# Two more modulation blocks as dot products, head norms and softmax rows scaled by ScalarE, and a new placing of side work

## The chip, the cores and the metric

The kernel runs on one core of one Trainium2 chip. The time is device microseconds of one execution. Three timed executions of the kernel before took 1323.88, 1324.15 and 1324.64 us, so the median is 1324.15 us. The profile comes from a fourth execution of its own.

The core has TensorE (PE for matmuls, PEld for their weight loads), VectorE (DVE), ScalarE (ACT), GpSimd (POOL) and SyncE (SP), which issues most of the loads. Each engine works through its own instructions in the order in which they stand and stops at the first one whose inputs or buffers are not there.

## What is computed

One layer of a diffusion backbone, for two groups of 128 tokens ("prompt" and "sample"), model width 2048. A conditioning vector per group gives six modulation vectors. The core of the reference:

```python
sh1, sc1, g1, sh2, sc2, g2 = ada_mod(c[:, None, :], w_ada[l], b_ada[l])   # split(silu(c) @ w_ada + b_ada, 6)
h = rms_norm(xs, norm1_w[l]) * (1 + sc1) + sh1
qa, ka, va, qb, kb, vb, ga, gb = project_heads(h, ...)    # h @ w_in, then rms_norm of every q and k head
qa, ka = axial_rope(qa, T), axial_rope(ka, T)             # sample group only
oa = latent_window_attention(qa, ka, va, cache_a_k, cache_a_v, sink)
ob = latent_neighbourhood_attention(qb, kb, vb, cache_b_k, cache_b_v, rpb_b)
xs = xs + g1 * merge_branches(oa, ob, ga, gb, w_br_a, w_br_b, w_out)
h2 = rms_norm(xs, norm2_w[l]) * (1 + sc2) + sh2
xs = xs + g2 * sq_relu_mlp(h2, w_up[l], w_down[l])
```

The prompt group runs through the same steps with plain attention over its own 128 tokens. Everything is 32-bit floating point.

## The kernel before

**Steps.** The large products (w_in, w_br_a, w_br_b, w_out, w_up, w_down) run as 456 steps in one list, `wsteps`. A step loads one 512 KB piece of a weight (`raw`, 128x1024). To keep the precision, the piece is split into a high part and a rest: ScalarE copies `raw` into `wH` (line 101), VectorE subtracts `wH` from `raw` into `wL` (line 260). TensorE then multiplies in threes, high by high, low by high and high by low. Outside the fast form of w_up a step has 12 matmuls of 512 columns. Steps 0 to 71 make q, k and v, 72 to 135 the gates, 136 to 167 the two branch products, 168 to 199 w_out, and the rest w_up and w_down.

**What sets the order.** Nothing is scheduled by itself. `run()` writes the instructions out step by step. The strings `RUN` and `LOOK` have one digit per step: how many steps ahead of the matmuls the load is issued, and how many ahead the split is written. All other work has step numbers in tables at the head of the file (`POST`, `JOBS`, `DOTS`, `DOTS2`, `DOTS1`, `SS_AT`, `T_PAIR`, `P_PAIR`), and is written behind the matmuls of that step. So a table entry decides where a piece of side work stands among the splits on ScalarE and VectorE. Tiles of 128x1024 come from one pool of 50 buffers.

**Splits with a DMA.** For the steps listed in `LO_DMA` VectorE does not make the rest. ScalarE writes minus `wH` into `wL` (line 266) and GpSimd issues a DMA that adds the weight from memory once more (line 267).

**Modulation.** The shift and scale of a norm are needed as columns. Each vector is 16 blocks of 128 columns, and a block can be made in two ways.
- As matmuls, in pairs of blocks: `pair_load` fetches 2 MB per block, `pair_mm` (line 330) issues 16 small matmuls per block, `ada_evac` copies the result out with ScalarE, `ada_cols` turns it with four PE transposes (line 348) and finishes with small VectorE operations (lines 351 to 358). For the second norm the blocks 0 to `FB_DVE`-1 go this way, at the steps in `SS_AT`.
- As dot products on VectorE: `dot` (line 1411) multiplies a transposed weight tile (`aT`, 512 KB) by the conditioning row spread over the partitions (`cB`), and sums. A block of shift and scale is 2 vectors x 2 halves x 2 groups, so 8 such operations and four loads. `DOTS` places these for gate 1 and for the second norm's blocks from `FB_DVE` on, `DOTS1` those of the first norm's last two blocks, `DOTS2` those of gate 2.

**Head norms.** `qk_stat` squares a unit of q or k heads on ScalarE, one instruction per group, and VectorE sums per head (line 673). GpSimd makes the inverse roots. `qk_apply` scales the prompt group's heads one by one on ScalarE (line 683) and the sample group's with one VectorE multiply (line 684). VectorE then applies the norm weight (686) and the rotary (693 to 696), and `qk_T` turns the result for the scores. There are six units of 4 heads per group and one (`kvA`) of 2. `POST` has the three steps of each.

**Softmax.** There are eight attention jobs, each of four heads and one group, with 128 keys per row for the prompt and 256 for the sample. `normalise` (line 795) divides the four heads' rows by their sums with one VectorE multiply. `JOBS` has the five steps of each job: scores, softmax, normalise, turning, values.

**The last steps.** `up_act`, `up_planes`, `up_flip` and `up_T` square the result of w_up, cut it into 16-bit planes, turn it with a transposing DMA and join it (`fTa`, then `a14H`, `a14L` for the last unit but one). `P_PAIR` and `T_PAIR` place them.

Of the kernel before, what the change touches and what calls it, by code (L numbers as in the profile page):

```python
# [14 lines left out]
AF = mybir.ActivationFunctionType  # L15
OP = mybir.AluOpType
AX = mybir.AxisListType

P = 128
D = 2048  # L20
KC = D // P
HD = 128
# [7 lines left out]
PIECES = [[2 * i, 2 * i + 1] for i in range(8)]  # L30
GEN = 50
LOAD = 4
FB_DVE = 6
FB1 = 14
H_AT = 41
DOTS1 = [26, 26, 29, 36, 39, 40, 41, 42]
CHUNKS = [2, 2, 2, 4, 6]
NFAST = 8
FAST = {1: (0, 2, 3, 5, 6, 7), 2: (0, 2, 3, 5, 6, 7), 3: (0, 2, 3, 5, 6, 7), 4: (0, 2, 3, 5, 6, 7), 5: (0, 2, 3, 5, 6, 7), 6: (0, 2, 3, 5, 6, 7), 7: (0, 2, 3, 5, 6, 7)}
# [8 lines left out]
GATE2_USE = 3  # L48
ROW_AT = [5, 5, 9, 5]
DIRECT = (3,)  # L50
LO_DMA = [88, 106, 116, 131, 165, 180, 184, 196, 218, 224, 230, 232, 250, 251, 256, 282, 283, 288, 314, 315, 320, 329, 346, 347, 352, 378, 379, 384, 392, 410, 416, 442, 443, 449, 450]
LO_AHEAD = 2

LOOK = "652322414122454322223333333122333442223323122555465644344534355765215632223444456685566655544323333333321122122312343545666445443333342344444444444434556566643344457766322234414766567565566546555331235663226676666666656665554444444444444444555555555555555544433333333344445555555555555555444444444444444455555555555555554444433244444444555555555555555546444444444444445555555555555555444444444445555555666465555555554444446656654585434443744464222433444444"
RUN = "411111111111121323334444433333333312222233465566655466545667777556664445555776765655445445555656776654432333333312444444555566553333333343334455555566655655555655666575565577788866677666665653476544343366555566666666666666665555555555554444566666666666666655555555555555556666666666666666555555555555555566666666555666665555577555555555666666666666666655555555555555556666666666666666555577755555575454566666676555566666666665555555776766555535444666666666"
CONST_AT = [65, 69]
ADA_AT = [None, 5, 13, 16, 21, 37, 32]
XS_AT = {1: 13, 2: 19, 3: 31}
POST = {('kvA', 0): [67, 71, 76], ('qA', 0): [70, 73, 78], ('qA', 1): [72, 74, 83], ('kB', 0): [76, 86, 90], ('qB', 0): [82, 84, 93], ('kB', 1): [87, 90, 98], ('qB', 1): [90, 93, 96]}
JOBS = [[80, 81, 81, 88, 94], [79, 83, 88, 90, 92], [87, 87, 89, 95, 100], [93, 93, 96, 102, 105], [96, 97, 100, 105, 112], [102, 103, 107, 112, 123], [105, 107, 111, 118, 123], [112, 115, 118, 121, 123]]  # L60
SS_AT = [44, 57, 75, 75, 139, 139]
T_AT = [3, 4]
PREP_IN = [5, 7]
DOTS = [32, 44, 47, 47, 49, 50, 51, 52, 53, 56, 58, 60, 67, 67, 68, 69, 77, 78, 84, 85, 92, 93, 93, 94, 95, 99, 100, 103, 103, 104, 108, 110, 111, 111, 116, 118, 120, 120, 121, 122, 126, 126, 128, 129, 130, 132, 134, 137, 137, 138, 138, 143, 144, 145, 151, 155, 155, 158, 160, 160, 166, 167, 173, 173, 174, 175, 176, 178, 179, 180, 183, 190]
DOTS2 = [234, 237, 240, 266, 269, 272, 298, 301, 329, 330, 332, 363, 364, 367, 397, 398, 424, 426, 426, 428, 429, 431, 431, 432, 432, 436, 439, 439, 440, 441, 444, 444]
STAT_AT = [-1, 0, 8, 11]
T_PAIR = [[6, 8], [6, 8], [8, 10], [5, 7], [10, 13], [8, 14], [12, 9]]
P_PAIR = [[1, 3], [2, 4], [3, 4], [-1, 3], [3, 4], [3, 6], [6, 4]]
M_TE = (3,)
M_AT = [1, 3, 8]  # L70
FLIP = 2
P_UP = [2, 3]
T_UP = [6, 11]
COL = {"qA": 0, "kvA": 1024, "qB": 1536, "kB": 2560, "vB": 3584, "gA": 4608, "gB": 6656}


# [1 line left out]
def tile_hybrid_step(ctx: ExitStack, tc: tile.TileContext, a):  # L78
# [98 lines left out]
    r = SM(2, "r")  # L177
# [489 lines left out]
    def qk_stat(u, nh):  # L667
        raw = units[u]
        sq = G("sq").rearrange("p (s h d) -> p s h d", s=2, d=HD)[:, :, 0:nh, :]
        for s in range(2):  # L670
            act.activation(sq[:, s].rearrange("p h d -> p (h d)"), raw[:, s, 0:nh * HD], AF.Square)
        ssq, r = SM(2 * nh, "ssq"), SM(2 * nh, "rq")
        dve.tensor_reduce(ssq.rearrange("p (s h) -> p s h", s=2), sq, axis=AX.X, op=OP.add)
        rsqrt(r, ssq, HD * EPS)
        qk[u] = sq, r

    def qk_apply(u, nh):

        name, raw = u[0], units[u]
        x4 = raw.rearrange("p s (h d) -> p s h d", d=HD)[:, :, 0:nh, :]  # L680
        sq, r = qk.pop(u)
        for h in range(nh):
            act.activation(x4[:, 0, h, :], x4[:, 0, h, :], AF.Copy, scale=r[:, h:h + 1])
        dve.tensor_tensor(x4[:, 1], x4[:, 1], r[:, nh:2 * nh].unsqueeze(2).to_broadcast([P, nh, HD]), op=OP.mult)
        if name in ("kvA", "kB"):
            dve.tensor_tensor(x4[:, 0], x4[:, 0], K2["wb"][name].unsqueeze(1).to_broadcast([P, nh, HD]), op=OP.mult)
        if name in ("qA", "kvA"):
# [44 lines left out]
    def att_job(mix, s, g):  # L732
        st = {}
        nb = 1 + s
        nk = P * nb
# [53 lines left out]
        def normalise():  # L789
            den, prob = st["den"], st["P"]  # L790
            if mix == "A":
                dve.tensor_tensor(den, den, st["es"], op=OP.add)
            rd = SM(4, "rd")
            dve.reciprocal(rd, den)
            dve.tensor_tensor(prob[:, :, 0:nk], prob[:, :, 0:nk], rd.unsqueeze(2).to_broadcast([P, 4, nk]), op=OP.mult)

        def probs_T():
            st["PT"] = G("probT").rearrange("p (b h q) -> p b h q", b=2, h=4)
# [808 lines left out]
```

## Time and profile before

| | us |
|---|---|
| median of three timed executions | 1324.15 |
| the profiled execution, its own time | 1324.28 |
| its span in the trace | 1322.5 |
| TensorE matmul busy | 1309.0 |
| VectorE busy | 1151.4 |
| ScalarE busy | 890.8 |
| GpSimd busy | 87.1 |

The span is 1.8 us shorter than the execution's own time. Busy times are sums over the span and say nothing about who waits for whom, since the stages differ: loads take the DMA engines' whole time for the first 200 us, VectorE is fullest between 160 and 260 us and between 1220 and 1300 us, and ScalarE between 920 and 1010 us and in the w_up stages. Matmul records overlap: one is shown for 390 ns, while the next begins after about 227 ns.

### The profile page before, as it was taken

What the parts mean: (1) busy time and instruction counts of PE and PEld (TensorE: products, weight loads), DVE (VectorE), ACT (ScalarE), POOL (GpSimd) and SP (SyncE); (2) the same over time, 40 slices, a digit from 0 to 9 for tenths busy, and PEclk for the clock granted to TensorE, in tenths of its full rate; (3) what the DMA queues carried; (4) which work ended last, traced back from release to release, by engine and by line L of the source; (5) the groups of instructions that cost most, each with busy time, mean ns of one, the idle gap of its engine ahead of it and who ended that gap; (6) DMA issues with size and microseconds to landing.
All of it is one profiled execution on the core that took longest, in us unless ns stands there. A gap on an engine that the chain in (4) does not pass through costs nothing.

```text
span 1322.5 us, 18220 instructions
## 1 busy us (share of the span) xinstructions
PE 1309.0 (99%) x6388; PEld 1061.3 (80%) x6388; DVE 1151.4 (87%) x1487; ACT 890.8 (67%) x1129; POOL 87.1 (7%) x109
## 2 busy tenths in 40 slices
PE   8999999999999999999999999999999999999998
PEld 4777788788888878888888888888888888888876
DVE  4578699988898999999789889898898998979996
ACT  5634656576565545755788877968879688796772
POOL 0000000512000000000100010100101001010011
PEclk9999999999999999999999999999999999999999
DMA  9999998887689999998489998888998799899996
GB/s 375 408 408 409 406 398 344 326 286 281 200 296 343 373 377 349 323 374 306 137 289 291 290 312 273 283 300 289 292 321 281 282 341 288 295 269 366 375 334 185
DMA packets 155260, 419.03 MB, mean 317 GB/s; under 512 B 52720, under 2 KB 53984, under 8 KB 155168
## 3 DMA queue, kind: packets, MB, share of 16 engines
q1 hardware_dynamic: 146128, 386.54, 80.1%
q0 software_dynamic: 8848, 31.23, 10.3%
q8 instruction: 50, 0.82, 0.2%
q14 instruction: 42, 0.34, 0.1%
q10 hardware_dynamic: 192, 0.10, 0.0%
HBM read 390.24 MB, written 17.61 MB: 308 GB/s over the span
## 4 chain that ended last, share of the span: by engine, by line
PE 93%; DMA 3%; DVE 2%; issue 1%; POOL 0%; ACT 0%; POOLq 0%; DVEq 0%; ACTq 0%
PE acc L313 16%; PE acc L314 16%; PE acc L315 16%; PE Q L1191 6%; PE Q L1192 6%; PE Q L1193 6%; PE acc L424 5%; PE acc L425 5%; PE acc L426 5%; PE ps_ada L330 2%; DMA araw<-in_w_pair 2%; PE ps_S L756 1%; DMA wL<-in_w_down 1%; DVE aT L1411 1%; PE acc L1026 1%
## 5 line engine op out<-in xcount | busy, mean ns | idle before, releaser
L101 ACT ACTIVATE wH<-raw 128x1024 fp32r<-128x1024 f32 (+1 forms) x376 | 381.0, 1045 | 126.4 <-DMA raw<-in_w_in 17.0
L260 DVE TENSOR_TENSOR wL<-raw,wH 128x1024 fp32r<-128x1024 f32 x335 | 399.1, 1223 | 47.8 <-ACT wH L101 32.7
L424 PE MATMUL acc<-wH,hH 128*128 128x512 f32 x276 | 109.1, 395 | 0.0
L426 PE MATMUL acc<-wH,hL 128*128 128x512 f32 x276 | 107.6, 390 | 0.0
L425 PE MATMUL acc<-wL,hH 128*128 128x512 f32 x276 | 107.5, 390 | 0.0
L313 PE MATMUL acc<-wH,hH 128*128 128x512 f32 x256 | 102.6, 401 | 0.0
L315 PE MATMUL acc<-wH,hL 128*128 128x512 f32 x256 | 99.8, 390 | 0.0
L314 PE MATMUL acc<-wL,hH 128*128 128x512 f32 x256 | 99.7, 390 | 0.0
L1411 DVE CUSTOM_DVE_ANT_0 junk<-aT,cB,cols 128x1024 bf16<-128x1024 f32 x56 | 71.3, 1283 | 1.4 <-DMA cB<-silu 1.4
L1411 DVE CUSTOM_DVE_ANT_0 aT<-aT,cB,cols 128x1024 f32<-128x1024 f32 x56 | 71.6, 1288 | 0.2
L424 PEld LDWEIGHTS acc<-wH,hH 128*128 128x128 f32 x276 | 51.8, 188 | 13.6 <-issue 3.3
L1256 DVE TENSOR_TENSOR tL<-t,tH 128x1024 fp32r<-128x1024 f32 x42 | 51.2, 1220 | 11.2 <-ACT tH L101 11.2
L426 PEld LDWEIGHTS acc<-wH,hL 128*128 128x128 f32 x276 | 51.8, 188 | 11.2 <-DVE hL L105 0.2
L101 ACT ACTIVATE uH<-raw 128x1024 fp32r<-128x1024 f32 x42 | 44.4, 1058 | 23.6 <-DVE raw L1250 21.5
L425 PEld LDWEIGHTS acc<-wL,hH 128*128 128x128 f32 x276 | 51.9, 188 | 10.3
L101 ACT ACTIVATE tH<-t 128x1024 fp32r<-128x1024 f32 x42 | 44.3, 1054 | 23.5 <-DVE t L1246 18.5
L313 PEld LDWEIGHTS acc<-wH,hH 128*128 128x128 f32 x256 | 48.1, 188 | 10.5 <-issue 1.1
L314 PEld LDWEIGHTS acc<-wL,hH 128*128 128x128 f32 x256 | 48.1, 188 | 10.0 <-issue 0.7
L315 PEld LDWEIGHTS acc<-wH,hL 128*128 128x128 f32 x256 | 48.1, 188 | 10.1
L1246 DVE TENSOR_TENSOR t<-raw 128x1024 f32<-128x1024 f32 x42 | 51.2, 1218 | 1.0 <-PE acc L314 1.0
L1238 DVE TENSOR_TENSOR XL<-raw,XH 128x1024 fp32r<-128x1024 f32 x42 | 51.2, 1218 | 0.6 <-DMA sm<-dsum 0.5
L1256 DVE TENSOR_TENSOR uL<-raw,uH 128x1024 fp32r<-128x1024 f32 x42 | 51.1, 1218 | 0.0
(630 smaller groups left out, 3374.4 us busy)
## 6 DMA issues: line engine op xcount, KB each, us to landing
raw<-in_w_in SPq DMA_DIRECT2D x133, 512.0 KB, 9.0
raw<-in_w_down SPq DMA_DIRECT2D x128, 512.0 KB, 6.6
raw<-in_w_upF SPq DMA_DIRECT2D x84, 512.0 KB, 6.3
araw<-in_w_pair SPq DMA_DIRECT2D x80, 512.0 KB, 10.1
aT<-in_w_gT SPq DMA_DIRECT2D x64, 512.0 KB, 8.9
aT<-in_w_adaT SPq DMA_DIRECT2D x48, 512.0 KB, 9.9
raw<-in_w_up SPq DMA_DIRECT2D x44, 512.0 KB, 6.2
raw<-in_w_out SPq DMA_DIRECT2D x32, 512.0 KB, 10.2
```

Source lines behind the costliest of these rows:

```text
L101: act.activation(out, in_, AF.Copy)
L260: dve.tensor_tensor(st["lo"], st["raw"], st["hi"].bitcast(F32), op=OP.subtract)
L313: pe.matmul(acc[tb], sh, wh[:, k, :], start=f, stop=False, **kw)
L314: pe.matmul(acc[tb], sh, wl[:, k, :], start=False, stop=False, **kw)
L315: pe.matmul(acc[tb], sl, wh[:, k, :], start=False, stop=l, **kw)
L424: pe.matmul(acc[tb], sh, wh[:, k, :], start=kt == 0 and k == 0 and not held and not seeded, stop=False, **kw)
L425: pe.matmul(acc[tb], sh, wl[:, k, :], start=False, stop=False, **kw)
L426: pe.matmul(acc[tb], sl, wh[:, k, :], start=False, stop=last and k == 1 and not hold, **kw)
L1191: pe.matmul(acc, stat[0], hi, start=f, stop=False)
L1192: pe.matmul(acc, stat[0], lo, start=False, stop=False)
L1256: dve.tensor_tensor(b[n + "L"], v, b[n + "H"].bitcast(F32), op=OP.subtract)
L1411: dve.tensor_tensor_reduce(out, box["raw"], cB[s, tag], 1.0, dst if second else baT[:, part, fb:fb + 1], OP.mult, OP.add, dst)
```

## The change

The second norm's blocks made by matmuls go from 6 to 4, so blocks 4 and 5 become dot products: 32 small matmuls, 4 transposes, one ScalarE copy, four small VectorE operations and 4 MB of loads go, and 16 dot products with 8 loads of 512 KB come. The squares of the head norms are taken head by head on ScalarE with the sum as a second output, and the VectorE sums go. The sample group's heads and the softmax rows are scaled by ScalarE, head by head. `LO_DMA` has 33 entries in place of 35. The strings `LOOK` and `RUN` differ in some places (the first of them is shown, cut), and most tables by a few entries.

```diff
-FB_DVE = 6
+FB_DVE = 4
-DOTS1 = [26, 26, 29, 36, 39, 40, 41, 42]
+DOTS1 = [26, 29, 34, 35, 35, 36, 39, 42]
-LO_DMA = [88, 106, 116, 131, 165, 180, 184, 196, 218, 224, 230, 232, 250, 251, 256, 282, 283, 288, 314, 315, 320, 329, 346, 347, 352, 378, 379, 384, 392, 410, 416, 442, 443, 449, 450]
+LO_DMA = [57, 92, 106, 114, 116, 127, 165, 172, 184, 196, 224, 232, 237, 256, 282, 283, 288, 314, 315, 320, 329, 346, 347, 352, 378, 379, 384, 385, 410, 416, 440, 442, 449]
-POST = {('kvA', 0): [67, 71, 76], ('qA', 0): [70, 73, 78], ('qA', 1): [72, 74, 83], ('kB', 0): [76, 86, 90], ('qB', 0): [82, 84, 93], ('kB', 1): [87, 90, 98], ('qB', 1): [90, 93, 96]}
+POST = {('kvA', 0): [67, 71, 76], ('qA', 0): [70, 73, 78], ('qA', 1): [72, 74, 83], ('kB', 0): [76, 86, 90], ('qB', 0): [80, 84, 93], ('kB', 1): [87, 91, 99], ('qB', 1): [90, 93, 96]}
-SS_AT = [44, 57, 75, 75, 139, 139]
+SS_AT = [75, 75, 139, 139]
-DOTS = [32, 44, 47, 47, 49, 50, 51, 52, 53, 56, 58, 60, 67, 67, 68, 69, 77, 78, 84, ...]
+DOTS = [43, 44, 47, 47, 48, 48, 50, 51, 52, 56, 57, 58, 60, 62, 67, 67, 68, 69, 69, 73, 78, 79, 84, ...]
...
     def qk_stat(u, nh):
...
+        ssq, r = SM(2 * nh, "ssq"), SM(2 * nh, "rq")
         for s in range(2):
-            act.activation(sq[:, s].rearrange("p h d -> p (h d)"), raw[:, s, 0:nh * HD], AF.Square)
-        ssq, r = SM(2 * nh, "ssq"), SM(2 * nh, "rq")
-        dve.tensor_reduce(ssq.rearrange("p (s h) -> p s h", s=2), sq, axis=AX.X, op=OP.add)
+            for h in range(nh):
+                act.activation(sq[:, s, h, :], raw[:, s, h * HD:(h + 1) * HD], AF.Square,
+                               accum_out=ssq[:, s * nh + h:s * nh + h + 1])
         rsqrt(r, ssq, HD * EPS)
...
     def qk_apply(u, nh):
...
-        for h in range(nh):
-            act.activation(x4[:, 0, h, :], x4[:, 0, h, :], AF.Copy, scale=r[:, h:h + 1])
-        dve.tensor_tensor(x4[:, 1], x4[:, 1], r[:, nh:2 * nh].unsqueeze(2).to_broadcast([P, nh, HD]), op=OP.mult)
+        for s in range(2):
+            for h in range(nh):
+                act.activation(x4[:, s, h, :], x4[:, s, h, :], AF.Copy, scale=r[:, s * nh + h:s * nh + h + 1])
...
         def normalise():
...
             dve.reciprocal(rd, den)
-            dve.tensor_tensor(prob[:, :, 0:nk], prob[:, :, 0:nk], rd.unsqueeze(2).to_broadcast([P, 4, nk]), op=OP.mult)
+            for h in range(4):
+                act.activation(prob[:, h, 0:nk], prob[:, h, 0:nk], AF.Copy, scale=rd[:, h:h + 1])
```

The functions' line numbers move by one to two, so the squares and scalings of lines 671 and 683 stand at 673 and 685 in the changed kernel, and the dot products are at line 1413. Three places in the order of the instructions follow, word for word, the kernel before first.

VectorE, from the head norm of `kvA` (line 673, the unit of mixer A's keys and values) to the split of step 76, which stands behind a pair of modulation blocks on TensorE:

```order
L673 TENSOR_REDUCE ssq<-sq 128x8
L684 TENSOR_TENSOR u_kvA_1989<-u_kvA_1989,rq 128x256
L686 TENSOR_TENSOR u_kvA_1989<-u_kvA_1989,early_76 128x256
L693 TENSOR_TENSOR sq<-u_kvA_1989,early_76 128x4x32 x2
L695 TENSOR_TENSOR u_kvA_1989<-u_kvA_1989,early_76 128x256
L696 TENSOR_TENSOR u_kvA_1989<-u_kvA_1989,sq 128x256
L673 TENSOR_REDUCE ssq<-sq 128x8
L684 TENSOR_TENSOR u_qA_1840<-u_qA_1840,rq 128x512
L693 TENSOR_TENSOR sq<-u_qA_1840,early_76 128x8x32 x2
L695 TENSOR_TENSOR u_qA_1840<-u_qA_1840,early_76 128x512
L696 TENSOR_TENSOR u_qA_1840<-u_qA_1840,sq 128x512
L260 TENSOR_TENSOR wL<-raw,wH 128x1024 x2
```

```order
L1413 ISA aT,shT_157<-aT,cB_1146,cols 128x1024
L1413 ISA shT_157 128x1
L687 TENSOR_TENSOR u_kvA_1970<-u_kvA_1970,early_76 128x256
L694 TENSOR_TENSOR sq<-u_kvA_1970,early_76 128x4x32 x2
L696 TENSOR_TENSOR u_kvA_1970<-u_kvA_1970,early_76 128x256
L697 TENSOR_TENSOR u_kvA_1970<-u_kvA_1970,sq 128x256
L1413 ISA junk,scT_158<-aT,cB_1144,cols 128x1024
L1413 ISA scT_158 128x1
L694 TENSOR_TENSOR sq<-u_qA_1817,early_76 128x8x32 x2
L696 TENSOR_TENSOR u_qA_1817<-u_qA_1817,early_76 128x512
L697 TENSOR_TENSOR u_qA_1817<-u_qA_1817,sq 128x512
L260 TENSOR_TENSOR wL<-raw,wH 128x1024 x2
```

Both sums and both multiplies are gone, and dot products (`ISA`, with a second row that reads the sum out) stand between the rotary of the units.

ScalarE, the same place, from the squares of the first `qA` unit to its scaling:

```order
L671 ACTIVATE sq<-u_qA_1840 128x512 x2
L101 ACTIVATE u_vB_2498<-acc 128x512 x2
L683 ACTIVATE u_kvA_1989<-u_kvA_1989,rq 128x128 x2
L671 ACTIVATE sq<-u_qA_1909 128x512 x2
L683 ACTIVATE u_qA_1840<-u_qA_1840,rq 128x128 x4
```

```order
L673 ACTIVATE sq,ssq<-u_qA_1817 128x128 x8
L101 ACTIVATE u_vB_2455<-acc 128x512 x2
L685 ACTIVATE u_kvA_1970<-u_kvA_1970,rq 128x128 x4
L673 ACTIVATE sq,ssq<-u_qA_1897 128x128 x8
L685 ACTIVATE u_qA_1817<-u_qA_1817,rq 128x128 x8
```

The order is the same; 2 squares became 8 with a sum each, and 2 or 4 scalings became 4 or 8.

ScalarE near the end, around the joining of `a14` (`fTa`, `a14H`) and the first steps of `w_down`'s last columns:

```order
L101 ACTIVATE wH<-raw 128x1024
L266 ACTIVATE wL<-wH 128x1024
L101 ACTIVATE wH<-raw 128x1024
L101 ACTIVATE fTa_11510<-pTa_11414 128x2x1024
L101 ACTIVATE a14H<-fTa_11510 128x1024
L101 ACTIVATE wH<-raw 128x1024
L266 ACTIVATE wL<-wH 128x1024
L101 ACTIVATE wH<-raw 128x1024 x3
```

```order
L266 ACTIVATE wL<-wH 128x1024
L101 ACTIVATE wH<-raw 128x1024
L101 ACTIVATE dsum_11531<-acc 128x512 x2
L101 ACTIVATE wH<-raw 128x1024
L266 ACTIVATE wL<-wH 128x1024
L101 ACTIVATE wH<-raw 128x1024
L101 ACTIVATE fTa_11561<-pTa_11451 128x2x1024
L101 ACTIVATE a14H<-fTa_11561 128x1024
L101 ACTIVATE wH<-raw 128x1024 x3
```

The second `L266`, the start of a split by DMA, stood behind the joining of `a14` and now stands ahead of it.

More of the change, by code (lines that the diff above doesn't have):

```diff
@@ L72 @@
 P_UP = [2, 3]
-T_UP = [6, 11]
+T_UP = [7, 12]
 COL = {"qA": 0, "kvA": 1024, "qB": 1536, "kB": 2560, "vB": 3584, "gA": 4608, "gB": 6656}
```

14 lines of the change are left out of this document (7 added, 7 removed).

## The prediction

> **What bounds the kernel now.** The page first: the span, the busy times, and the chain of work that ended last, by engine.
>
> ```profile
> span 1322.5 us, 18220 instructions
> PE 1309.0 (99%) x6388; PEld 1061.3 (80%) x6388; DVE 1151.4 (87%) x1487; ACT 890.8 (67%) x1129; POOL 87.1 (7%) x109
> ...
> PE 93%; DMA 3%; DVE 2%; issue 1%; POOL 0%; ACT 0%; POOLq 0%; DVEq 0%; ACTq 0%
> ```
>
> A busy PE need not be a PE at its pace, so the view by windows comes next, with TensorE alone (start and end, length, busy time with matmuls, granted clock, DMA share, GB/s).
>
> ```profile
> 680.00:1200.00 520.00, 520.00 (x2296) 1.00 0.91 294
> ```
>
> 2296 matmuls in 520 us are one per 226.5 ns at a granted clock of 1.00, without a gap. A step of 12 takes 2.72 us. The same pitch is seen in the stages before. So TensorE's own work sets the time, and a microsecond taken from it is worth a microsecond, until TensorE reaches something that isn't ready. The question is how close the other engines stand behind it. Three stages, with all engines:
>
> ```profile
> 160.00:260.00 100.00, 100.00 (x490) 81.09 (x489) 95.19 (x139) 60.22 (x87) 19.41 (x18) 1.00 0.92 356
> 260.00:340.00 80.00, 80.00 (x457) 65.54 (x456) 70.20 (x107) 55.52 (x114) 13.50 (x12) 1.00 0.83 299
> 1220.00:1300.00 80.00, 77.15 (x338) 62.72 (x337) 79.54 (x109) 54.32 (x60) 7.34 (x11) 1.00 1.03 344
> ```
>
> The columns behind the length are PE, PEld, DVE, ACT and POOL. VectorE is 95% full from 160 to 260 us, just where the removed matmuls stand, and has half a microsecond free from 1220 to 1300 us. ScalarE has 24.5 us free from 260 to 340 us.
>
> **What leaves TensorE.** The first two blocks of the second norm, one by one, and their transposes, with the matmuls around them:
>
> ```profile
> 171.31 0.39 PE L426 MATMUL acc<-wH,hL 128*128 128x512 f32 x1
> 171.63 1.93 PE L330 MATMUL ps_ada<-araw,early 128*32 128x256 f32 x32
> ...
> 173.83 0.40 PE L425 MATMUL acc<-wL,hH 128*128 128x512 f32 x1
> ...
> 208.76 0.39 PE L426 MATMUL acc<-wH,hL 128*128 128x512 f32 x1
> 209.08 1.93 PE L330 MATMUL ps_ada<-araw,early 128*32 128x256 f32 x32
> ...
> 211.28 0.40 PE L425 MATMUL acc<-wL,hH 128*128 128x512 f32 x1
> ...
> 213.57 0.39 PE L426 MATMUL acc<-wH,hL 128*128 128x512 f32 x1
> 213.80 0.60 PE L348 MATMUL ps_sel<-ident,S 128*128 128x128 f32 x4
> ...
> 214.47 0.40 PE L425 MATMUL acc<-wL,hH 128*128 128x512 f32 x1
> ```
>
> From 171.31 to 173.83 us are 2.52 us, of which two ordinary pitches are 0.45, so a block costs 2.07 us, the second one too. The transposes cost 0.90 - 0.45 = 0.45 us. Together **4.59 us** leave. Bounds: by busy time alone, 2 x 1.93 + 0.60 = 4.46; both ends are near.
>
> **What VectorE gets and loses.** The rows around step 76, the split behind the next pair of blocks. First VectorE, then TensorE.
>
> ```profile
> 219.19 0.36 DVE L620 TENSOR_SCALAR early<-early 128x384 f32<-128x384 f32 x1 [2.02 <-DMA early<-in_k_norm_b]
> ...
> 247.97 1.27 DVE L1411 CUSTOM_DVE_ANT_0 aT<-aT,cB,cols 128x1024 f32<-128x1024 f32 x1
> ...
> 249.17 1.27 DVE L1411 CUSTOM_DVE_ANT_0 junk<-aT,cB,cols 128x1024 bf16<-128x1024 f32 x1
> ...
> 254.26 0.42 DVE L686 TENSOR_TENSOR u_kvA<-u_kvA,early 128x256 f32<-128x256 f32 x1 [1.02 <-ACT u_kvA L683]
> ...
> 260.73 2.36 DVE L260 TENSOR_TENSOR wL<-raw,wH 128x1024 fp32r<-128x1024 f32 x2 [0.34 <-PE acc L315]
> ```
>
> ```profile
> 260.62 3.66 PE L330 MATMUL ps_ada<-araw,early 128*32 128x256 f32 x64
> ...
> 264.55 0.40 PE L314 MATMUL acc<-wL,hH 128*128 128x512 f32 x1
> ```
>
> The operations that VectorE gives up, by form:
>
> ```profile
> L673 DVE TENSOR_REDUCE ssq<-sq 128x8 f32<-128x1024 f32 x6 | 7.3, 1217 | 2.2 <-ACT sq L671 2.2
> L684 DVE TENSOR_TENSOR u_kB<-u_kB,rq 128x512 f32<-128x512 f32 x2 | 1.4, 686 | 0.0
> L795 DVE TENSOR_TENSOR prob<-prob,rd 128x1024 f32<-128x1024 f32 x4 | 4.9, 1224 | 0.1
> L795 DVE TENSOR_TENSOR prob<-prob,rd 128x512 f32<-128x512 f32 x4 | 2.8, 692 | 0.1
> ```
>
> A dot product costs 249.17 - 247.97 = 1.20 us, so 16 cost 19.2, and the two splits that `LO_DMA` hands back cost some 1.2 each (2.36 for two). Against these 21.6 stand 7 sums (7.3 and half of one, 0.6), 7 multiplies (six of 0.69 and half of one, 4.5) and 8 scalings (7.7), together 20.1. Over the kernel that is even; the place matters. The dot products come early, the relief late. By the order VectorE has, up to the split of step 76, 55 dot products where it had 48, and 3 sums, 2 multiplies, 1 split and four small operations less: 7 x 1.20 - (2 x 1.22 + 0.6) - (0.69 + 0.35) - 1.2 - 0.5 = 2.6 us more.
>
> That split ended at 260.73 + 1.2 = 261.95 us and was needed at 264.55 us, so it was 2.6 us early. In the change TensorE is there at 264.55 - 4.59 = 259.96 us. VectorE would end it at 261.95 + 2.6 = 264.6 us, less the idle time before it that its fuller queue covers: 2.02, 1.02 and 0.34 us in the rows above, 3.4 in all. So TensorE waits between 1.2 and 4.6 us. I take **1.6 us**, near the low end: a constant load does not come later because VectorE comes later, the kvA scaling is on ScalarE some five dot products ahead of its use, and the third wait is for TensorE, which is earlier. Waits at earlier splits count in the same 1.6, because a TensorE that has waited once comes later to the next. From there on the sums and scalings that left give VectorE room.
>
> **What ScalarE gets.** The prices, from the timeline of ScalarE and from groups by form:
>
> ```profile
> 261.75 0.97 ACT L683 ACTIVATE u_qA<-u_qA,rq 128x128 f32<-128x128 f32 x3
> ...
> 268.46 1.16 ACT L671 ACTIVATE sq<-u_kB 128x512 f32<-128x512 f32 x2
> ...
> 286.10 0.37 ACT L781 ACTIVATE prob<-ps_S,nm 128x128 f32<-128x128 f32 x1
> ...
> 287.49 0.21 ACT L787 ACTIVATE es<-es 128x4 f32<-128x4 f32 x1
> ```
>
> ```profile
> L101 ACT ACTIVATE wH<-raw 128x1024 fp32r<-128x1024 f32 x53 | 54.6, 1061 | 20.6 <-PE acc L314 7.8 <-DMA raw<-in_w_in 6.0 <-PE ps_qT L709 2.6
> L768 ACT ACTIVATE prob<-ps_S 128x256 f32<-128x256 f32 x4 | 1.4, 385 | 0.0
> ```
>
> A 128x128 scaling in a row costs 0.29 us (three in 0.97, the last one's 0.39 in full). A square with a sum is not in the trace; the nearest row is the exponential with a sum, four between 286.10 and 287.49, 0.35 each. Its floor is the scaling's 0.29, its ceiling twice that. So 52 squares cost 18.2 (15.1 to 30.2) in place of 7 pairs, 7.6; 26 more scalings cost 7.5; 32 softmax scalings cost 16 x 0.29 + 16 x 0.385 = 10.8. That is about 29 us more, nearly all between 250 and 420 us. From 260 to 340 us I count four units' squares (4 x 1.7), five units' scalings (5 x 1.2) and four jobs (5.4), 18 us: ScalarE's 55.5 of 80 become 73.5. Its largest idle group there is the one before `wH` copies, 20.6 us, in which ScalarE waits for buffers and loads, being ahead. How far ahead, by the windows of tile `wH` (TensorE's uses, eight a step, and ScalarE's copies):
>
> ```profile
> 0.00:340.00 340.00, 250.99 (x783) 146.82 (x784) 119.67 (x102) 104.14 (x105) 1.00 0.94 364
> ```
>
> 783 uses are 97.9 steps, 105 copies less three for the first steps' halves are 102: 4.1 steps, 11 us ahead. The new waits stand here: each softmax scaling waits for VectorE's reciprocal, and behind it in ScalarE's queue stand the next `wH` copies, for which VectorE's splits and then TensorE wait. I take **0.2 us** (0 to 10, the rival below).
>
> **What moves at the end.** TensorE stands still twice, with ScalarE's rows before the second stop:
>
> ```profile
> 1272.01 0.50 PE L315 MATMUL acc<-wH,a14L 128*128 128x512 f32 x1 [1.10 <-DVE a14L L890]
> 1282.05 0.50 PE L314 MATMUL acc<-wL,a15H 128*128 128x512 f32 x1 [1.69 <-DMA wL<-in_w_down]
> ```
>
> ```profile
> 1266.39 2.56 ACT L101 ACTIVATE fTa<-pTa 128x2048 uint16<-128x2048 uint16 x1 [1.62 <-DMA pTa<-pla]
> ...
> 1271.02 1.06 ACT L266 ACTIVATE wL<-wH 128x1024 fp32r<-128x1024 f32 x1
> ```
>
> The DMA split of step 443 began at 1271.02 us, because ScalarE first waited for the transposing DMA and joined `a14`. In the change `LO_DMA` has 440 and 442 there, and both starts stand ahead of the joining. So the 1.69 us go. The 1.10 us before `a14L` stay, its chain being as it was. VectorE gets one split more (1.2 us) in a stage that is full, from nothing to 1.2 us lost; I take half. Net **-1.1 us** (-1.7 to +1.2). The 4 MB of loads for two blocks that go and the 4 MB of dot product tiles that come are even, and GpSimd has two DMAs less on its queue. I put both at nothing, since the loads run ahead of their use; without that cover 4 MB at the 356 GB/s of the first window above would be 12 us.
>
> **Sum.** Against the profiled execution's own 1324.28 us: -4.59 + 1.6 + 0.2 - 1.1 = -3.9, so **1320.4 us**. The profiled execution is 0.13 us above the median of the timed ones, which is left in the rounding.
>
> **The rivals.**
> *ScalarE becomes the bound from 260 to 340 us (slower).* With 18 us more, and if ScalarE keeps all its 24.5 us of waiting because the waits are for TensorE's transposes and VectorE's maxima and not for being ahead, it ends the stage 18 us later. It was 11 us ahead, and TensorE comes 3 us sooner, so TensorE waits 10 us: 1320.2 + 10 = 1330 us. It turns the sign when ScalarE keeps about 19 of the 24.5 us. For it: in-order waits between ScalarE and VectorE double in each job. Against it: 20.6 us of idle time are before `wH` copies. Chance 0.20.
> *VectorE takes it all back (no change).* Nothing of the 3.4 us of idle time is recovered, TensorE waits 4.6 us at step 76, and with the end's gain halved the time is 1324.28 - 4.59 + 4.6 - 0.6 = 1323.7 us. For it: 95% full. Against: three waits with causes of their own. Chance 0.18.
> *TensorE has time to spare (no change).* Its weight loads are busy for 80% of the span. If that, and not the matmuls, measured its load, a fifth of its time would be free and the 4.59 us would buy nothing: 1324.28 - 1.1 = 1323.2 us. Against it: the pitch of 226.5 ns does not vary over 520 us. Chance 0.03. The Trainium skill, Perfetto Trace Analysis, section Identifying the Most-Contended Engine, gives this rule: it calls matmul busy time a poor measure of a matmul engine's headroom and takes LDWEIGHTS busy time instead.
> *All hidden (faster still).* No wait at step 76 and none at the end beyond 1.10: 1324.28 - 4.59 - 1.69 = 1318.0 us. Chance 0.12.
>
> **How the numbers follow.** The forecast has 0.47; its own range is 1318.8 to 1322.3 us. Up to 0.2%, 2.6 us, cannot be told from no change: 1321.5 to 1326.8 us. Faster is the last rival and 0.44 of the forecast, 0.56. No change is 0.03 of the forecast, the second and third rival and 0.01 of the first, 0.25. Slower is the rest of the first, 0.19. The range of 8 in 10 runs from 1317.3, below the best case, to 1327.0, which leaves out most of the first rival.
>
> **What would show it.** In the changed profile: no group on line 330 between 155 and 230 us; a TensorE wait for VectorE's split behind the pair that stood at 260.62 us, about 1.6 us long; no wait of TensorE for `wH` from 260 to 420 us; ScalarE near 74 of 80 us in that first stage; one stop near the end in place of two. Wrong would be a forecast that meets `wH` waits of several us there, a stop of over 4 us at step 76, or a new stop among the w_up steps, where I expect none.

## The result, and the profile after

The changed kernel takes 1321.88 us (median of 20 runs, 1320.67 to 1323.64) beside 1323.93 us for the kernel before on the same chips (20 runs, 1322.10 to 1326.20). The ratio is 0.9985, 95% interval 0.9979 to 0.9991: some 2 us faster, which is less than the 0.2% that was set as the bound of no change. The forecast was 1320.4 us. The time lies in the forecast's own range (1318.8 to 1322.3 us), but by that bound it counts as no change, to which the prediction gave 0.25, and not as faster, to which it gave 0.56. The profiled executions took 1324.28 and 1321.69 us, with 2.9 us between their spans; what follows explains those 2.9 us. The page of the changed kernel: span, busy times, and the chain of work that ended last.

```profile
span 1319.6 us, 18243 instructions
PE 1305.4 (99%) x6319; PEld 1059.7 (80%) x6320; DVE 1152.2 (87%) x1494; ACT 913.3 (69%) x1273; POOL 87.2 (7%) x107
...
PE 72%; DMA 4%; DVE 3%; ACT 1%; issue 0%; SPq 0%; POOL 0%; ACTq 0%; DVEq 0%
```

TensorE's busy time is 3.6 us lower, VectorE's is what it was, ScalarE's 22.5 us higher. The shares of the chain cannot be set beside those of before: followed back from the end, it breaks off at 243.8 us, so its shares sum to 80%. Where it breaks off it is on VectorE, whose dot products and splits it follows from there to the split that TensorE waits for at 262 us. The windows that the prediction used, of the changed kernel (start and end, length, then PE, PEld, DVE, ACT and POOL busy, granted clock, DMA share, GB/s):

```profile
160.00:260.00 100.00, 98.90 (x471) 80.51 (x473) 93.75 (x137) 65.18 (x127) 22.23 (x19) 1.00 0.89 337
260.00:340.00 80.00, 79.39 (x422) 65.42 (x411) 63.37 (x98) 68.65 (x201) 13.33 (x12) 1.00 0.87 319
300.00:320.00 20.00, 20.00 (x112) 17.25 (x111) 8.73 (x17) 20.00 (x75) 5.02 (x6) 1.00 0.83 301
680.00:1200.00 520.00, 520.00 (x2296) 430.77 (x2295) 464.56 (x513) 416.55 (x455) 28.44 (x40) 1.00 0.89 291
1220.00:1300.00 80.00, 78.55 (x343) 63.48 (x342) 79.07 (x109) 51.49 (x57) 6.51 (x10) 1.00 1.01 335
```

The stage from 680 to 1200 us is what it was to the last matmul. TensorE now stands still in the first two windows, where before it was 100% busy. ScalarE is full to the last tenth from 300 to 320 us, and TensorE does not notice. The stops, from TensorE's timeline of the changed kernel (start, duration, what it waited for in brackets):

```profile
217.59 0.39 PE L424 MATMUL acc<-wH,hH 128*128 128x512 f32 x1
218.54 0.50 PE L425 MATMUL acc<-wL,hH 128*128 128x512 f32 x1 [0.57 <-DVE wL L260]
...
220.49 0.39 PE L424 MATMUL acc<-wH,hH 128*128 128x512 f32 x1
...
222.09 0.50 PE L425 MATMUL acc<-wL,hH 128*128 128x512 f32 x1 [0.54 <-DVE wL L260]
...
257.47 4.00 PE L330 MATMUL ps_ada<-araw,early 128*32 128x256 f32 x64
261.40 0.50 PE L313 MATMUL acc<-wH,hH 128*128 128x512 f32 x1
262.38 0.51 PE L314 MATMUL acc<-wL,hH 128*128 128x512 f32 x1 [0.47 <-DVE wL L260]
...
1268.45 0.50 PE L313 MATMUL acc<-wH,a14H 128*128 128x512 f32 x1 [0.54 <-ACT a14H L101]
...
1269.71 0.50 PE L315 MATMUL acc<-wH,a14L 128*128 128x512 f32 x1 [0.53 <-DVE a14L L892]
```

Three stops for VectorE's splits are new, and at the end the two stops of 1.10 and 1.69 us have become several of half a microsecond. Set against each other by the start of the same matmul, the two traces give this account (us, after less before):

| up to | difference so far | what happened there |
|---|---|---|
| 55 us | -0.2 | |
| 212 us | -4.9 | the two blocks and the transposes are gone: -4.7 |
| 277 us | -2.0 | the three stops at 218, 222 and 262 us: +2.5; the pair of blocks ahead of the third takes 4.00 us where it took 3.66: +0.3 |
| 501 us | -2.6 | a wait of the gate's transposes for their column, 0.5 us, is gone |
| 1214 us | -2.7 | nothing |
| the end | -2.9 | several small stops in place of two: -0.2 |

The 4.7 us left TensorE as computed. More than half came back within 65 us. Why, VectorE's timeline shows, of the changed kernel, around the first of the three stops:

```profile
210.04 1.28 DVE L1413 CUSTOM_DVE_ANT_0 junk<-aT,cB,cols 128x1024 bf16<-128x1024 f32 x1
211.25 0.08 DVE L1413 DVE_READ_ACCUMULATOR2_ANT gc_g<- 128x1 f32 x1
215.85 0.36 DVE L620 TENSOR_SCALAR early<-early 128x384 f32<-128x384 f32 x1 [4.52 <-DMA early<-in_k_norm_b]
...
217.20 0.17 DVE L633 TENSOR_SCALAR sink<-sink 128x8 f32<-128x8 f32 x1
217.27 1.22 DVE L260 TENSOR_TENSOR wL<-raw,wH 128x1024 fp32r<-128x1024 f32 x1
218.41 1.28 DVE L1413 CUSTOM_DVE_ANT_0 aT<-aT,cB,cols 128x1024 f32<-128x1024 f32 x1
```

VectorE stands still for 4.52 us before the head norms' constants (2.02 us before the change), and the split that TensorE waits for at 218 us stands behind them in its queue. This DMA wait, and not the amount of VectorE's work, became the first theory for the loss.

### The profile page after: what moved, and what is told of

It reads as the page before. It is cut to its first block, busy times and chain, and to the rows that moved or that the text cites. A ratio compares the mean times of both kernels' runs of the same rounds, so it can differ in the third digit from the quotient of the medians.

```text
span 1319.6 us, 18243 instructions
## 1 busy us (share of the span) xinstructions
PE 1305.4 (99%) x6319; PEld 1059.7 (80%) x6320; DVE 1152.2 (87%) x1494; ACT 913.3 (69%) x1273; POOL 87.2 (7%) x107
## 4 chain that ended last, share of the span: by engine, by line
PE 72%; DMA 4%; DVE 3%; ACT 1%; issue 0%; SPq 0%; POOL 0%; ACTq 0%; DVEq 0%
PE acc L314 15%; PE acc L313 15%; PE acc L315 15%; PE Q L1194 6%; PE Q L1193 6%; PE Q L1195 6%; DMA raw<-in_w_down 2%; DMA aT<-in_w_gT 1%; DMA pTa<-pla 1%; PE ps_S L757 1%; DVE wL L260 1%; DVE aT L1413 1%; DVE junk L1413 1%; PE acc L1026 1%; PE acc L1027 1%; PE acc L1028 1%
## 5 line engine op out<-in xcount | busy, mean ns | idle before, releaser
L1413 DVE CUSTOM_DVE_ANT_0 junk<-aT,cB,cols 128x1024 bf16<-128x1024 f32 x60 | 77.0, 1295 | 0.0
L1413 DVE CUSTOM_DVE_ANT_0 aT<-aT,cB,cols 128x1024 f32<-128x1024 f32 x60 | 76.6, 1289 | 0.1
L1258 DVE TENSOR_TENSOR tL<-t,tH 128x1024 fp32r<-128x1024 f32 x42 | 51.3, 1220 | 6.3 <-ACT tH L101 6.3
L1248 DVE TENSOR_TENSOR t<-raw 128x1024 f32<-128x1024 f32 x42 | 51.2, 1220 | 4.1 <-PE acc L315 3.2
L1240 DVE TENSOR_TENSOR XL<-raw,XH 128x1024 fp32r<-128x1024 f32 x42 | 51.2, 1220 | 0.2 <-DMA raw<-in_w_upF 0.2
```

What stands on the lines that cost most here:

```text
L1258: dve.tensor_tensor(b[n + "L"], v, b[n + "H"].bitcast(F32), op=OP.subtract)
L1413: dve.tensor_tensor_reduce(out, box["raw"], cB[s, tag], 1.0, dst if second else baT[:, part, fb:fb + 1], OP.mult, OP.add, dst)
```

## The experiments

Twelve kernels, in four groups that were each timed beside the kernel before on one chip (medians 1323.3 to 1323.8 us). Ratios are to that kernel, with 95% intervals.

**1. The two blocks taken away and nothing put in their place.** The edit, to the kernel before:

```diff
-    for c in range(FB_DVE // 2):
+    for n in range(2):
+        pool.memset(mod[1][n][:, 0:2, :], 0.0)
+    for c in range(1, FB_DVE // 2):
         box = {}
```

> The kernel before without its first two blocks of the second norm: no matmuls on line 330 for them, no transposes, no loads of their weights, and no dot products in their place; those four columns of the norm's scale and shift are left at zero. Theory (the gain is the matmuls; what is given back comes from VectorE having to wait for the constants of the head norms and from its fuller queue): TensorE does 4.6 us less, VectorE gets nothing more, so little is given back; 1319.4 to 1320.4 us beside the 1323.9 of before, with a stop of at most 1 us near step 76. Rival (VectorE stands so close behind that whatever TensorE gains there is lost again at step 76): 2 us or more of stops there, 1321.4 us or more.

1320.15 us, ratio 0.9973 (0.9963 to 0.9983): -3.7 us. One stop between 200 and 480 us is listed, for a split of VectorE, none near step 76:

```profile
208.62 0.50 PE L425 MATMUL acc<-wL,hH 128*128 128x512 f32 x1 [0.81 <-DVE wL L260]
```

Set against the trace of before by the start of the same matmul, the 4.6 us leave as the pitch says, and 1.5 us of them have come back by 217 us: 1.1 at this stop, and 0.4 in two gaps near 175 us that are too short to be listed. So VectorE is close behind even with no dot product more. Near the end this trace gains 2.0 us again, 1.7 of them because the stop of 1.69 us is gone, with all tables as before. The kernel also loads 4 MB less, which this run does not separate. It settles the third rival: weight loads are 80% busy here too (`PEld 1058.9 (80%)`), and a microsecond taken from TensorE still shortened the run. The Trainium skill, Perfetto Trace Analysis, section Identifying the Most-Contended Engine, judges a matmul engine's headroom by LDWEIGHTS busy time, beside the share of peak arithmetic that is reached (MFU). Read by the first alone, as the rival reads it, a fifth of TensorE's time would be free; the measurement says no.

**2. The constants' DMAs earlier.** The edit, to the changed kernel (`load_consts_in` is the first part of `load_consts`: the five DMAs for the rope table, the three weights and the sink):

```diff
-    def load_consts():
+    K1 = []
+
+    def load_consts_in():
...
+        K1.extend([rc, wb, sk])
+
+    def load_consts():
+        rc, wb, sk = K1
...
+    load_at(CONST_AT[0] - 5, load_consts_in)
     load_at(CONST_AT[0], load_consts)
```

> The changed kernel, with the DMAs of the head norms' constants (rope, the three weights, the sink) issued five steps earlier, ahead of five loads of w_in and one of w_gT; VectorE's operations on them stay at their place. In the changed kernel VectorE stands still 4.52 us before them. Theory (this wait, not the number of dot products, makes the three stops of TensorE at 218, 222 and 262 us): VectorE is some 4 us earlier from there on, the three stops go, 2.2 us less than the changed kernel, 1319.7 us. Rival (VectorE is late at 262 us because it has 2.6 us more work): the two stops at 218 and 222 go, the one at 262 us stays or takes over what they held; 1321 us or more.

1319.04 us, ratio 0.9963 (0.9950 to 0.9975), 2.8 us less than the changed kernel, and that is just the 2.5 and 0.3 us of the account above. VectorE's timeline at the same place:

```profile
209.88 1.28 DVE L1420 CUSTOM_DVE_ANT_0 junk<-aT,cB,cols 128x1024 bf16<-128x1024 f32 x1
...
211.09 0.36 DVE L628 TENSOR_SCALAR early<-early 128x384 f32<-128x384 f32 x1
...
212.51 1.22 DVE L260 TENSOR_TENSOR wL<-raw,wH 128x1024 fp32r<-128x1024 f32 x1
```

The wait is gone, the split starts 4.76 us earlier than in the changed kernel, and TensorE's waits from 150 to 1250 us come down to one that both kernels have:

```profile
PE ps_h L1069 <- DVE h2f L1061: 0.6, 1, 0.6
```

All 16 dot products are still where they were. The rival, which had the stop at 262 us stay because of VectorE's work, falls: that stop was the late end of the same wait, 45 us on.

**3. The same edit on the kernel before** (three steps earlier).

> The kernel before, with the DMAs of the head norms' constants issued three steps earlier. Theory (that wait costs time only where a split behind it is needed at once; before, TensorE does not stop between 200 and 480 us for VectorE): VectorE's 2.02 us of standing still shrink and the time stays, 1323.9 us within 0.7. Rival (constants that come early save time by themselves, as 2.8 us in the changed kernel): 1322.5 us or less.

1324.22 us, ratio 1.0003 (0.9994 to 1.0012). VectorE's 2.02 us of standing still are gone from its timeline, and nothing is gained. A wait on VectorE costs nothing until a split that is needed at once stands behind it. The change had made TensorE 4.7 us earlier and that split only 3.5 us (220.72 and 217.27 us).

**4. ScalarE's part alone.** The three hunks of the diff in `qk_stat`, `qk_apply` and `normalise`, on the kernel before, all tables as before:

```diff
-            act.activation(sq[:, s].rearrange("p h d -> p (h d)"), raw[:, s, 0:nh * HD], AF.Square)
+            for h in range(nh):
+                act.activation(sq[:, s, h, :], raw[:, s, h * HD:(h + 1) * HD], AF.Square,
+                               accum_out=ssq[:, s * nh + h:s * nh + h + 1])
...
-            dve.tensor_tensor(prob[:, :, 0:nk], prob[:, :, 0:nk], rd.unsqueeze(2).to_broadcast([P, 4, nk]), op=OP.mult)
+            for h in range(4):
+                act.activation(prob[:, h, 0:nk], prob[:, h, 0:nk], AF.Copy, scale=rd[:, h:h + 1])
```

> The kernel before, with only the head norms and the softmax rows scaled by ScalarE; six blocks stay matmuls and all tables are those of before. Theory (ScalarE's 29 us are free, and relief for VectorE alone buys nothing, since TensorE does not wait for VectorE there): within 1 us of 1323.9, no new wait of TensorE for wH between 250 and 420 us. Rival (the added ScalarE work delays the wH copies): 1326 us or more, with waits for wH there.

1330.17 us, ratio 1.0049 (1.0035 to 1.0063): 6 us slower. The theory falls in this form. But the rival's place is wrong too: TensorE never waits for `wH`. It waits once, for ScalarE's copy of the transposed probabilities. TensorE's timeline and ScalarE's, of this kernel:

```profile
319.67 0.39 PE L315 MATMUL acc<-wH,hL 128*128 128x512 f32 x1
323.12 1.13 PE L811 MATMUL ps_o<-probT,u_kvA 128*128 128x512 f32 x2 [3.06 <-ACT probT L101]
```

```profile
317.77 2.47 ACT L685 ACTIVATE u_kB<-u_kB,rq 128x128 f32<-128x128 f32 x8
320.11 0.33 ACT L673 ACTIVATE sq<-u_qB 128x128 f32<-128x128 f32 x1
...
322.45 1.10 ACT L101 ACTIVATE probT<-ps_PT 128x512 f32<-128x512 f32 x2
```

Eight scalings of `u_kB` (2.47 us) and eight squares of `u_qB` stand just ahead of the copy, and two jobs' softmax scalings not far before them. In its profiled execution, at 1328.32 us, the kernel is 4.0 us longer than before; 3.3 of these arise at this stop. The other 2 us of the median are not in the trace. The two executions with a mean granted clock of 0.999 took 1328.3 and 1328.9 us, the three with 0.996 to 0.998 took 1330.2 to 1331.6 us. So they go with a lower clock; that it fell behind this stop, as it does behind longer ones (last section), is not shown.

**5. The same, with the steps of the norms and of the attention jobs as in the change.** The edit to the kernel of 4 (of `POST` and `JOBS`, the entries that matter at this place):

```diff
-POST = {..., ('qB', 0): [82, 84, 93], ('kB', 1): [87, 90, 98], ...}
-JOBS = [[80, 81, 81, 88, 94], [79, 83, 88, 90, 92], [87, 87, 89, 95, 100], ...]
+POST = {..., ('qB', 0): [80, 84, 93], ('kB', 1): [87, 91, 99], ...}
+JOBS = [[80, 81, 82, 88, 94], [79, 83, 88, 90, 94], [87, 87, 88, 95, 100], ...]
```

> The kernel before with the head norms and softmax rows on ScalarE, and with POST and JOBS (the steps of the head norms and of the attention jobs) as in the change. With the tables of before it took 1330.2 us, with a stop of 3.2 us before ps_o at 323 us, where ScalarE's copy of probT was late. Theory (ScalarE's extra work is free only because the change placed this work anew): the stop goes, 1324 to 1326.5 us. Rival (ScalarE is too full there in any order): a stop of 2 us or more stays between 300 and 350 us, 1327 us or more.

1324.10 us, ratio 1.0002 (0.9993 to 1.0011). The stop is gone: the scaling of `u_kB` now stands behind the copy, and the values of the second job two steps later.

```profile
318.19 1.07 ACT L101 ACTIVATE probT<-ps_PT 128x512 f32<-128x512 f32 x2
319.15 2.46 ACT L685 ACTIVATE u_kB<-u_kB,rq 128x128 f32<-128x128 f32 x8
```

So ScalarE's work is free only with the tables that came with it: the entries of `POST` and `JOBS`, which the prediction passed over, are worth 6 us by the medians, and 4.4 us between the profiled executions.

**6 to 8. The relief undone on the changed kernel**: all of it, the head norms alone, the softmax rows alone. Each undoes the hunks of 4, with all tables as changed.

> The changed kernel, with the head norms' sums and scalings and the softmax rows' scaling as in the kernel before (half or all of it on VectorE). Theory (the relief is what lets the 16 early dot products fit): some 20 us come back to VectorE between 235 and 420 us, the stop near step 76 grows from 0.75 to 3 or 4 us and others follow; 1324 to 1328 us. Rival (VectorE has room for it, the relief is worth nothing): 1321.9 us as the changed kernel.

1327.60 us, ratio 1.0029 (1.0017 to 1.0040).

> The changed kernel with the head norms as in the kernel before (sums and half of the scalings on VectorE); the softmax rows stay with ScalarE. The kernel with neither took 1327.6 us. Theory (what counts of the relief is what lies ahead of the split of step 76: two and a half sums and one and a half multiplies, 4.1 us): the stop near step 76 is 4 to 5 us as there, 1326 to 1328 us. Rival (the softmax scaling is the relief that counts): within 1 us of the changed kernel's 1321.9.

1326.93 us, ratio 1.0024 (1.0015 to 1.0033).

> The changed kernel with the softmax rows scaled by VectorE as before; the head norms stay with ScalarE. Eight operations, 7.7 us, go back to VectorE between 290 and 420 us, where it has 24 us free in the changed kernel; 10.8 us leave ScalarE. Theory (of the relief only the head norms count, since only they lie ahead of a split that is late): within 1 us of the changed kernel's 1321.9. Rival (VectorE needs both reliefs): 1324 us or more, with stops of TensorE for wL between 290 and 420 us.

1321.31 us, ratio 0.9982 (0.9973 to 0.9991). TensorE's wait for the split of step 76, of the three kernels in this order (each has 0.4 to 1.0 us of waits near 220 us beside it):

```profile
PE acc L314 <- DVE wL L260: 4.3, 1, 4.3
```

```profile
PE acc L314 <- DVE wL L260: 4.0, 1, 4.0
```

```profile
PE acc L314 <- DVE wL L260: 0.5, 1, 0.5
```

The head norms are the whole relief, 5 us, by way of what lies ahead of the split at step 76. With them back on VectorE that split starts at 264.74 us, 3.6 us later than in the changed kernel (261.11). Not all of the 5 us are this work: 1.5 us of run 7, and 2.7 us of run 6, arise behind the stop, where the granted clock is lowered (last section). The softmax rows moved 32 operations onto ScalarE and gained nothing.

**9. The end: the list of DMA splits alone.** The edit, to the changed kernel:

```diff
-LO_DMA = [..., 410, 416, 440, 442, 449]
+LO_DMA = [..., 410, 416, 442, 443, 449, 450]
```

> The changed kernel with the last entries of LO_DMA as before (442, 443, 449, 450 in place of 440, 442, 449), so GpSimd's DMA makes one split more and VectorE one fewer. Theory (the shorter list removed the stop of 1.69 us before step 443's split, and paid for it with the small stops of the last 60 us): a stop of over 1 us for wL from in_w_down is back and the stops of 0.3 and 0.5 us go; 1322.4 to 1323.6 us. Rival (which steps the list names does not matter there): 1321.9 us within 0.5.

1329.01 us, ratio 1.0041 (1.0029 to 1.0054): 7 us slower than the changed kernel, and neither theory had it. ScalarE's timeline:

```profile
1256.99 1.06 ACT L101 ACTIVATE dsum<-acc 128x512 f32<-128x512 f32 x2
1266.58 1.06 ACT L101 ACTIVATE wH<-raw 128x1024 fp32r<-128x1024 f32 x1 [8.52 <-DMA pTa<-pla]
...
1272.09 1.06 ACT L101 ACTIVATE a14H<-fTa 128x1024 fp32r<-128x1024 f32 x1
```

A copy into `wH` waits 8.52 us for the transposing DMA that reads `pla`, with which it has no data in common. ScalarE's instructions with their waits, of this kernel and of the changed one:

```
983 L101 ACTIVATE wH<-raw 128x1024 [waits DMAHW7_49,DMAHW3_49]
```

```
984 L101 ACTIVATE wH<-raw 128x1024 [waits DMAHW3_49]
```

`DMAHW3` is its own load, `DMAHW7` the one that `fTa` waits for as well, the transposing DMA. The reading that fits is that the buffers of the pool go round: one split more or fewer ahead of it moves later tiles to other buffers, and this `wH` fell on the one that `pla` held. The programs built from the two kernels bear it out: here this `wH` and the `pla` of `a14` have one address, in the changed kernel they have two. Behind it wait the joining of `a14` and then TensorE, 5.7 us.

**10. All tables of the end as before**, on the kernel of 2:

```diff
-LO_DMA = [..., 440, 442, 449]
-P_PAIR = [..., [6, 5]]
+LO_DMA = [..., 442, 443, 449, 450]
+P_PAIR = [..., [6, 4]]
```

with `LOOK` and `RUN` from step 420 and `DOTS2` as before.

> The changed kernel with the constants' DMAs issued five steps earlier (1319.0 us with its four stops of together 2.4 us in the last 65 us), and with the tables of the tail as before: LO_DMA from 442 on, LOOK and RUN from step 420, DOTS2 and the sixth pair of P_PAIR. LO_DMA alone put a wH into the buffer that the transposing DMA still read and cost 7 us; with all of them the order of buffers is that of before. Theory (the tail of before has two stops, for a14L and for the DMA's split; the second went in the kernel without the first two blocks, whose TensorE was 5 us early as here): one stop of 1.3 us, 1317.9 us. Rival (both stops come back): 2.9 us, 1319.5 us.

1318.19 us, ratio 0.9963 (0.9950 to 0.9975). TensorE's waits from 1220 us on:

```profile
PE acc L314 <- DMA wL<-in_w_down: 1.0, 1, 1.0
PE acc L315 <- DVE a14L L899: 0.5, 1, 0.5
PE acc L313 <- ACT a14H L101: 0.3, 1, 0.3
```

The wait for the buffer is gone, and the stop for the DMA's split is back, shorter. The medians of 2 and 10 are 0.85 us apart, their profiled executions 0.2 us the other way (1318.26 and 1318.44 us), and their intervals are the same, so which of the two ends is better is not settled; neither theory is right in its size.

**11. The bias earlier**, on the kernel of 2, to see why VectorE is slow from 234 to 246 us:

```diff
-CONST_AT = [65, 69]
+CONST_AT = [65, 58]
```

> The changed kernel with the constants' DMAs five steps earlier, and with the load of the bias at 58 in place of 69, so that GpSimd's eight selects on it run some 25 us earlier than from 234 to 246 us. In those 12 us VectorE's dot products took 1.49 us and its splits 1.5 us, elsewhere 1.20 and 1.13. Theory (VectorE is slowed by GpSimd's selects): the slow stretch moves with the selects, and between 234 and 246 us a dot product takes 1.20 us; the time stays near 1319. Rival (something else at that place slows VectorE): 1.49 us there still.

1319.47 us, ratio 0.9974 (0.9964 to 0.9985): the time is that of 2. The slow stretch went with GpSimd's selects. First VectorE in the kernel of 2, beside the selects; then GpSimd's second select in this kernel, with VectorE at the selects' new place and at their old one:

```profile
237.72 1.55 DVE L1420 CUSTOM_DVE_ANT_0 aT<-aT,cB,cols 128x1024 f32<-128x1024 f32 x1
...
239.20 1.55 DVE L1420 CUSTOM_DVE_ANT_0 junk<-aT,cB,cols 128x1024 bf16<-128x1024 f32 x1
```

```profile
203.72 1.42 POOL L660 TENSOR_SCALAR_AFFINE_SELECT bias<-bias 64x384 f32<-64x384 f32 x1
```

```profile
210.57 1.56 DVE L1420 CUSTOM_DVE_ANT_0 aT<-aT,cB,cols 128x1024 f32<-128x1024 f32 x1
...
212.06 1.55 DVE L1420 CUSTOM_DVE_ANT_0 junk<-aT,cB,cols 128x1024 bf16<-128x1024 f32 x1
...
238.66 1.28 DVE L1420 CUSTOM_DVE_ANT_0 aT<-aT,cB,cols 128x1024 f32<-128x1024 f32 x1
...
239.86 1.28 DVE L1420 CUSTOM_DVE_ANT_0 aT<-aT,cB,cols 128x1024 f32<-128x1024 f32 x1
```

Beside the selects a dot product takes 239.20 - 237.72 = 1.48 us in the one kernel and 212.06 - 210.57 = 1.49 in the other; at 238.66 us, with the selects moved away, 1.20.

**12. What the runs bear out, together**: the constants earlier, the end's tables as before, the softmax rows on VectorE. It is the sum of the edits of 2, 8 and 10.

> The three edits that the runs bear out together: the changed kernel with the constants' DMAs five steps earlier (-2.8 us), the tables of the tail as before (-0.8), and the softmax rows scaled by VectorE (-0.6, within the noise). Theory (VectorE has room between 290 and 420 us once it no longer stands still at 211 us, so the three add up): 1317.6 to 1318.2 us, no stop between 200 and 1260 us. Rival (the softmax scaling on VectorE makes its splits late again between 290 and 420 us): 1319 us or more.

1317.79 us, ratio 0.9958 (0.9944 to 0.9971), 5.5 us less than before. TensorE's longest wait from 150 to 1260 us is 0.6 us. Of the 5.5 us, 4.7 are the matmuls; that the constants' edit is needed to keep them is shown, that the other two edits add anything is within the noise.

## Why the prediction was right, and where its steps were not

**TensorE sets the time: right.** The pitch of 226.5 ns held, and 4.59 us was the right price. The pair of blocks that stays started at 260.62 us before and at 257.47 us in the change, 3.15 us earlier. The two stops that lie ahead of it in the change cost 0.86 us each; with them it is 4.9 us, of which 0.2 were there at 55 us. The 4.7 us left are the price and 0.1.

**VectorE's price, 1.6 us: within its bounds of 1.2 to 4.6, wrong in cause.** It was 2.8 us, 2.5 of them in three stops, and only the last of these at the split of step 76. The prediction put the whole loss there, down to 2.6 us more work ahead of it less the idle time that this work would cover, the 2.02 us before the constants among it, and said that "a constant load does not come later because VectorE comes later". The load did not come later. VectorE reached its operation 5.8 us earlier than before (211.3 and 217.2 us), and the load only 3.3 us earlier (215.9 and 219.2). By its groups up to there, its queue held the same 37 dot products, and one split and four small operations fewer; the seven dot products more all stand behind the constants. So the wait grew from 2.02 to 4.52 us, where the sum counted on it to be covered; that is the step that failed. The two other idle times, 1.02 and 0.34 us, are gone as it took them to be. Run 2 shows that the wait was enough to make all three stops, with the seven dot products in place.

**The work taken off VectorE: right for the norms.** The prediction counted 4.1 us of sums and multiplies ahead of step 76. Run 7 measures 3.6 us there.

**ScalarE, 0.2 us: right result, for a reason that does not carry.** It was argued that ScalarE is 11 us ahead with `wH`. Run 4 has that lead too (six steps at 317 us by the same count) and loses 6 us, in a copy of probabilities at which nobody looked. The slower rival (0.20) had the right engine, and the wrong victim; what kept it away was `POST` and `JOBS`, which the prediction did not cost at all. The size was too high: 22.5 us more work was measured where 29 were put. A square with its sum was put at 0.35 us, and takes 0.29, its floor (rows of the changed kernel):

```profile
304.05 0.32 ACT L673 ACTIVATE sq<-u_kB 128x128 f32<-128x128 f32 x1
...
304.34 0.32 ACT L673 ACTIVATE sq<-u_kB 128x128 f32<-128x128 f32 x1
```

52 times 0.06 us are 3.1, and the two DMA splits fewer take two more copies of 1.06 us off ScalarE; some 1.3 us of the difference stay open. From 260 to 340 us it is 68.65 us busy, not 73.5.

**The end, -1.1 us: wrong.** The forecast was one stop fewer. The trace shows -0.2 us: the stop of 1.69 us went, the 1.10 us before `a14L`, which were to stay, became 0.53, and stops for `a14H`, for splits and for the seeds of the last accumulators took their place. That the 1.69 us went because both starts stand ahead of the joining is not shown: in run 1 they are gone too, with the order of before. The step that failed is reading the end from the order of one list. Runs 9 and 10 show that the list cannot be taken apart from the other tables, because it moves the buffers of everything behind it.

**Not seen: 0.5 us** from the gate's transposes, which no longer wait for their column at 493 us.

Together the sum gave 1.2 us too little to VectorE and promised 0.9 too much at the end; 0.5 not seen, 0.2 for ScalarE and some 0.4 of smaller things went the other way. That is the 1.0 us between the -3.9 of the forecast and the -2.9 between the spans. The medians are only 2.05 us apart; the other 0.8 us are in no trace. That the forecast came within 1.5 us of the median is in part luck: what it had not seen or put too high took 1.1 us off its errors.

## What to carry to other kernels

When work leaves the engine that sets the time, look up what else becomes late there by name: each idle row of the neighbouring engines that ends on a DMA is a wait that the faster engine runs into, and issuing that DMA a few steps earlier cost nothing here and was worth 2.8 us, more than the change itself. "That engine has room" is not an argument until every instruction of it on which the bound engine waits has been looked at, not only the most frequent one. A table that names steps also moves buffers, so an entry is costed with the tables it was made with, or measured.

## What the runs showed of the hardware

A short stop of TensorE costs more than the wait listed for it. Behind the wait of 0.57 us at 218.54 us the ninth matmul after the row at 217.59 us starts at 220.49 us; nine pitches of 226.5 ns would have put it at 219.63. So 0.86 us went. Part of this is how the list counts: the wait begins where the record of the matmul before ends, 0.39 us after its start and 0.16 us behind the pitch; and the matmul behind the stop has 0.34 us to itself, 0.11 more than the pitch. The three waits of 0.57, 0.54 and 0.47 us sum to 1.58 us, and the stops cost 2.5.

A long stop costs more again, by the clock. TensorE alone, in 5 us behind the stop of 4.3 us in run 6, the stop of 4.0 us in run 7 and the stop of 3.06 us in run 4 (the granted clock is the third number from the end):

```profile
265.00:270.00 5.00, 4.76 (x11) 0.50 1.03 419
```

```profile
266.00:271.00 5.00, 4.99 (x19) 0.66 1.03 420
```

```profile
323.00:328.00 5.00, 4.88 (x19) 1.00 0.48 162
```

At 0.50 a matmul comes every 0.43 us in place of 0.23. By the start of the same matmul, TensorE falls back by 2.7 us more in run 6 and by 1.5 us more in run 7 before the clock is 1.00 again. Behind the stop of 5.7 us in run 9 the clock falls too, to 0.56 from 1273 to 1278 us. Behind 3.06 us it stays at 1.00. At what length between it begins, no run shows.

VectorE's dot product takes 1.49 us in place of 1.20 while GpSimd's selects run, and a select takes 1.4 to 1.5 us, about as long as the operation beside it; run 11 shows that the one causes the other. While VectorE stands idle a select takes 0.56 us, as in the kernel of run 3:

```profile
234.73 0.56 POOL L658 TENSOR_SCALAR_AFFINE_SELECT bias<-bias 64x384 f32<-64x384 f32 x1 [222.21 <-DMA raw<-in_w_in]
```

Eight selects cost VectorE some 2.4 us. The Trainium skill, SBUF — State Buffer, section SBUF: two separate sides, says that a VectorE operation with two inputs in SBUF and a GpSimd operation that reads SBUF exclude each other for a whole instruction, by ports that they share. The runs agree in that each slows the other; that VectorE loses 0.29 us to a select that takes 0.56 us alone is not explained by them.
